# State step of an S5 and attention trunk with the chunks stationary, joined value blocks, a gate bias kept as one row, and read-out matrices built a block ahead

## The chip, the core and the metric

The kernel runs on one core of a Trainium2 chip. A time is the device time of one execution in microseconds (us). The engines are TensorE (PE: matmuls, and transposes through the matmul array), VectorE (DVE), ScalarE (ACT), GpSimd (POOL, here a DMA queue and nothing else) and SyncE (SP, a second DMA queue). PE writes into eight PSUM banks of 128 partitions by 512 fp32 values; ACT and DVE read them. The profile tells for every stretch which clock TensorE was granted, as a share of 2.4 GHz: 1.00 is 2.4 GHz, 0.50 is 1.2 GHz.

## What is computed

512 tokens of width 2048 go through two layers. Cut to what matters here:

```python
for l in range(2):
    shift, scale, gate = split(silu(c) @ w_ada[l] + b_ada[l], 3)
    h = rms_norm(x, norm_g[l]) * (1 + scale) + shift
    u, z_s, q, k, v, z_a = split(h @ w_in[l])             # six times 1024 columns
    # S5: 64 groups of 16 channels, each with a 64-dim complex diagonal state
    states = associative_scan(a_bar, b_bar @ u)           # along the 512 tokens
    y = gelu((c_mat @ states).real + d_skip * u)
    y_s = glu(y) * silu(z_s)
    # 8 heads, difference of two softmax maps, causal
    y_a = head_norm((softmax(q1 k1) - lam * softmax(q2 k2)) @ v) * silu(z_a)
    x = x + gate * (concat(y_s, y_a) @ w_out[l])
out = rms_norm(x, final_g)
```

## The kernel before

**Big matmuls.** Every weight is used in three products of split fp32 numbers (high by high, high by low, low by high). Weights come as units of 128 x 1024 values, 144 for a layer, numbered through. `stream_ahead` (L308) loads a unit on SP's queue, ACT copies its high part (`hi`), DVE subtracts that from the unit (`lo`). There are four `hi`/`lo` pairs, so a unit is split four units ahead of its use and no sooner.

**One step per unit.** `step` (L255) writes out, in this order: a phase, the split of a later unit, the copies that empty the last step's bank (`evacs`), a phase, the matmuls of this unit, a phase. In each of the three phases every background generator moves on by one `yield`; `idle(n)` is n steps of nothing. So a generator's instructions stand at a fixed place between units on each engine, and an engine that is late makes the others wait there. Nothing is reordered later.

**Order of a layer** (L1198): columns of u, blocks of values, columns of z, then for 8 heads k, q and z_a with attention running behind them, then the GLU and the output projection. In the value blocks (`v_step`, L1223) the tokens' tiles are stationary and 256 weight columns move: a unit is 48 matmuls. In u and z the weights are stationary and 512 tokens move: 24 matmuls for a unit. Units are counted from 0: layer 0 has value blocks in units 24 to 31 and z in 32 to 47, layer 1 has values in 144 to 147, u in 148 to 163, values again in 164 to 175 and z in 176 to 191. `v_out` copies four PSUM banks (list `VB`) through two buffers and stores them to `vD`. The first z column writes to bank 1, then 0, then 7.

**State part** (`s5_state_gen`, L771). The 512 tokens are 64 chunks of 8 for every group. For block j of 8 groups, 8 fp32 matmuls give the chunks' state input in bank 3: the matrix B (128 x 128 for a group) is stationary, the chunks `U` (128 x 64) move; one step later ACT copies the bank into the state array `X`. A scan over the chunks follows: jobs of ACT swap, four DVE operations, one job a step, three levels up and three down. Then `PR` is scaled (`CS_SG1`, L855), the first read-out matrices are loaded (`be`, `kD`, `u` on POOL's queue), `idle(2)`, and eight read-out steps: DVE builds `O` (three operations of 1024) and masks `Mb` (one), PE runs 16 matmuls into bank 3 or 2, one step later DVE and ACT compute the gelu of that bank, and one step after that PE turns the result by four transposes. In the order of instructions on DVE the build of block j comes ahead of the gelu of block j-1.

**Bias of the modulation.** `ada_gen` (L524) brings the rows of w_ada as a background task on SP's queue and multiplies on DVE; for the gate the bias of 2048 values is first loaded to all 128 partitions (1 MB) on POOL's queue, and `ada_out` adds PSUM and bias on DVE.

Helpers: `q.act` L126, `q.tt` L129, `q.ts` L134, `q.stt` L138, `q.dma` L141 (POOL's queue), `q.mm` L144, `q.tr` L152. An fp32 matmul is two MATMUL records in the trace, one of the split products or a transpose is one.

Of the kernel before, what the change touches and what calls it, by code (L numbers as in the profile page):

```python
# [338 lines left out]
def build(ctx, tc, io):  # L339
# [169 lines left out]
    def ada_out(l, c):  # L509
        b = bank[4]  # L510
        if c < 8:
            k0 = 4 * (c % 4)
            f_o, s_o = mod_o[l]
            bb = pc(PP_BA + 32 * l + 16 * (c // 4) + k0, 4)
            if c < 4:
                q.tt(v(s_o + k0, 4), b[:, 0:4], bb, A)
            else:
                q.tt(v(f_o + k0, 4), b[:, 0:4], bb, A)
                q.stt(v(f_o + k0, 4), v(f_o + k0, 4), 1.0, pc(PP_NG + 16 * l + k0, 4), A, M)
        else:  # L520
            g0 = gl.gate + (c - 8) * 512
            q.tt(v(g0, 512), b, v(g0, 512), A)

    def ada_gen(l, chunks, ring, per, gate=False, late=0):  # L524
# [8 lines left out]
        if gate:  # L533
            q.dma(v(gl.gate, D), io["bgate"][l].partition_broadcast(P))
# [236 lines left out]
    def s5_state_gen(l):  # L771

        o = S5[l]
        todo = got = 0
        while o.v < 8:
            yield
            if todo > o.v:
# [3 lines left out]
            if got < 8 and o.d > got and o.v >= got - 1:  # L781
# [24 lines left out]
        for (ar, ai), (br, bi) in zip(pw, pw[1:]):  # L806
# [4 lines left out]
            q.stt(bi, ar, 2.0, ai, M, M)  # L811
        jobs = []
# [7 lines left out]
        for i, job in enumerate(jobs):  # L820
            if job is None:
# [35 lines left out]
        def load_m(j):  # L857
            base = q.kD[l][16384 * j:16384 * (j + 1)]
            src = bass.AP(base.tensor, base.offset, [[16, P], [2048, 8], [1, P]])
            q.dma(o.B[j % 2].rearrange("p (g f) -> p g f", g=8), src)  # L860

        s5_load_be(l, 0, 128)
        load_m(0)
        s5_load_u(l, 0)
        yield from idle(2)
# [20 lines left out]
        for j in range(8):  # L886
            if j < 7:
                s5_load_be(l, j + 1, 128)
                load_m(j + 1)
                s5_load_u(l, j + 1)  # L890
            be = v(s5.BE[j % 2], 384).rearrange("p (f g q) -> p f g q", f=3, g=8)
            O = o.A[j % 2]
            On4 = O.rearrange("p (g s e) -> p g s e", g=8, s=8)
            T4 = o.T.rearrange("p (g s e) -> p g s e", g=8, s=8)
            pr = PR[:, 8 * j:8 * j + 8, :].unsqueeze(3).to_broadcast([P, 8, 8, 16])
            pi = PI[:, 8 * j:8 * j + 8, :].unsqueeze(3).to_broadcast([P, 8, 8, 16])
            q.tt(On4, pr, be[:, 1].unsqueeze(2).to_broadcast([P, 8, 8, 16]), M)
            q.tt(T4, pi, be[:, 2].unsqueeze(2).to_broadcast([P, 8, 8, 16]), M)
            q.tt(O, O, o.T, SUB)
# [298 lines left out]
    def layer(l):  # L1198
# [11 lines left out]
        def v_out(b, st, cb):  # L1210
            t = v2(ut_o[vn[0] % 2], 256)
            vn[0] += 1
            q.act(t, b, AF.Copy)
            q.dma(q.vD[l][st * P:(st + 1) * P, cb * 256:(cb + 1) * 256], t)

        VB = (2, 7, 0, 1, 5, 6) if l == 0 else (0, 1, 2, 7, 5, 6)

        def v_bank(st, cb):
            i = 4 * (cb - (2 if l == 0 else 1)) + st
            assert i < 4 or o.r == 8  # L1220
            return bank[VB[i % 6]][:, 0:256]

        def v_step(un, cb, kc):  # L1223
            def pe():
                wh, wl = q.unit(un)

                for st in (2, 3, 1, 0) if l > 0 and cb == 1 and kc == 0 else range(4):
                    rows3(v_bank(st, cb), st, wh, wl, range(4 * kc, 4 * kc + 4), 256, kc == 0, kc == 3)

            def evac():  # L1230
                for st in range(4):
                    v_out(v_bank(st, cb), st, cb)

            q.step(pe, evac if kc == 3 else None)
# [59 lines left out]
        if l == 0:  # L1294
# [13 lines left out]
        for cb in range(first_cb, 4):  # L1308
            for kc in range(4):
                v_step(un, cb, kc)  # L1310
# [3 lines left out]
        for j in range(8):  # L1314
            b = bank[(1, 0, 7)[j % 3]]
# [288 lines left out]
def _layout(x, c, positions, norm_g, w_ada, b_ada, w_in, w_out, ssm_a_re, ssm_a_im, ssm_b_re, ssm_b_im,  # L1604
# [13 lines left out]
    for l in range(DEPTH):  # L1618
# [5 lines left out]
        def put_v(u, cb):  # L1624
            m = wv[:, :, 256 * cb:256 * (cb + 1)].reshape(4, 4, P, 256)
            w[u:u + 4] = m.transpose(0, 2, 1, 3).reshape(4, P, 1024)
            return u + 4

        if l == 0:
# [99 lines left out]
```

## Time and profile before

| | |
|---|---|
| median of 3 runs | 1918.66 us (1918.45 to 1919.98) |
| the profiled execution | 1919.61 us, of which the span is 1917.8 us |
| PE busy | 1883.1 us, 98% of the span |
| DVE busy | 1350.5 us, 70% |
| ACT busy | 788.0 us, 41% |
| mean granted clock | 0.993 |

PE is busy nearly all the time, so each microsecond of matmul taken out, and each wait of PE taken out or put in, is a microsecond of the kernel. DVE's 70% is a mean: there are stretches in which it is full. A timeline row is the start of an instruction (or of a run of equal ones, x16 is sixteen), its duration with its tail, engine, line, operation, output and inputs, size; in square brackets how long the engine had been idle and who ended that. Matmuls overlap, so what a matmul costs is read as the distance of starts.

### The profile page before, as it was taken

What the parts mean: (1) busy time and instruction counts of PE and PEld (TensorE: products, weight loads), DVE (VectorE), ACT (ScalarE), POOL (GpSimd) and SP (SyncE); (2) the same over time, 40 slices, a digit from 0 to 9 for tenths busy, and PEclk for the clock granted to TensorE, in tenths of its full rate; (3) what the DMA queues carried; (4) which work ended last, traced back from release to release, by engine and by line L of the source; (5) the groups of instructions that cost most, each with busy time, mean ns of one, the idle gap of its engine ahead of it and who ended that gap; (6) DMA issues with size and microseconds to landing.
All of it is one profiled execution on the core that took longest, in us unless ns stands there. A gap on an engine that the chain in (4) does not pass through costs nothing.

```text
span 1917.8 us, 27929 instructions
## 1 busy us (share of the span) xinstructions
PE 1883.1 (98%) x10440; PEld 1590.0 (83%) x10440; DVE 1350.5 (70%) x2590; ACT 788.0 (41%) x1489; POOL 200.8 (10%) x316
## 2 busy tenths in 40 slices
PE   7999999999999999999999999999999999999998
PEld 4678998878888888888898899888788888888887
DVE  7747867997788887769876434797687787653444
ACT  4333234445445554322254224444355445432222
POOL 0003220230000000100001220033000000000000
PEclk8999999999999999999999999999999999999999
DMA  9967652776656865777544433377766684455233
GB/s 354 403 254 245 185 154 86 218 201 213 182 181 192 221 192 176 264 264 245 170 160 136 130 114 114 99 228 200 205 188 191 181 219 122 123 168 202 94 92 118
DMA packets 120696, 358.77 MB, mean 187 GB/s; under 512 B 32272, under 2 KB 32848, under 8 KB 118128
## 3 DMA queue, kind: packets, MB, share of 16 engines
q1 hardware_dynamic: 97776, 277.14, 45.3%
q0 software_dynamic: 22784, 79.84, 14.0%
q8 instruction: 82, 1.34, 0.3%
q14 instruction: 54, 0.44, 0.1%
HBM read 309.60 MB, written 30.54 MB: 177 GB/s over the span
## 4 chain that ended last, share of the span: by engine, by line
PE 74%; DVE 13%; DMA 6%; issue 4%; ACT 3%; POOL 0%; SPq 0%; ACTq 0%; DVEq 0%; POOLq 0%
PE bk L145 72%; DVE sb L130 4%; DVE lo L130 3%; DVE sb L139 3%; PE bk L153 2%; DMA sb<-in_wada 1%; DMA sb<-in_w 1%; DVE ss L130 1%; ACT hi L127 1%; DMA x<-in_x 1%; DMA sb<-in_ssm_d 1%; ACT sb L127 1%; DMA sb<-sb 1%; DVE sb L134 1%; DMA vD<-sd 0%
## 5 line engine op out<-in xcount | busy, mean ns | idle before, releaser
L130 DVE TENSOR_TENSOR lo<-sb,hi 128x1024 fp32r<-128x1024 f32 x288 | 351.0, 1221 | 361.5 <-ACT hi L127 339.2
L127 ACT ACTIVATE hi<-sb 128x1024 fp32r<-128x1024 f32 x288 | 303.6, 1058 | 518.7 <-PE bk L145 394.6
L145 PE MATMUL bk<-hth,hi 128*128 128x512 f32 x1280 | 513.5, 401 | 0.0
L145 PE MATMUL bk<-hth,lo 128*128 128x512 f32 x1280 | 500.9, 391 | 0.0
L145 PE MATMUL bk<-htl,hi 128*128 128x512 f32 x1280 | 500.2, 391 | 0.0
L145 PE MATMUL bk<-hi,hth 128*128 128x256 f32 (+1 forms) x1088 | 360.1, 331 | 4.4 <-ACT hth L127 4.0
L145 PE MATMUL bk<-lo,hth 128*128 128x256 f32 (+1 forms) x1088 | 356.0, 327 | 0.5 <-DVE lo L130 0.5
L145 PE MATMUL bk<-hi,htl 128*128 128x256 f32 (+1 forms) x1088 | 356.1, 327 | 0.0
L139 DVE SCALAR_TENSOR_TENSOR sb<-sb 128x512 f32<-128x512 f32 (+7 forms) x633 | 295.5, 473 | 21.4 <-DMA sb<-in_wada 2.0
L145 PEld LDWEIGHTS bk<-hth,lo 128*128 128x128 f32 x1280 | 241.3, 188 | 51.8
L145 PEld LDWEIGHTS bk<-htl,hi 128*128 128x128 f32 x1280 | 241.9, 189 | 49.2 <-issue 1.9
L145 PEld LDWEIGHTS bk<-hth,hi 128*128 128x128 f32 x1280 | 241.6, 189 | 48.7 <-issue 2.3
L130 DVE TENSOR_TENSOR sb<-sb 128x4 f32<-128x4 f32 (+8 forms) x455 | 219.3, 499 | 29.5 <-DMA sb<-sb 12.5
L145 PEld LDWEIGHTS bk<-hi,hth 128*128 128x128 f32 x1088 | 207.1, 190 | 34.5 <-issue 12.3
L145 PEld LDWEIGHTS bk<-hi,htl 128*128 128x128 f32 x1088 | 207.0, 190 | 18.2 <-DVE htl L130 0.5
L145 PEld LDWEIGHTS bk<-lo,hth 128*128 128x128 f32 x1088 | 207.3, 191 | 17.4 <-DVE lo L130 0.7
L145 PE MATMUL bk<-gt,hi 128*128 128x512 f32 x512 | 159.4, 392 | 0.0
L145 PE MATMUL bk<-sb 128*128 128x128 f32 (+6 forms) x932 | 134.1, 340 | 4.8 <-DVE sb L433 3.9
L127 ACT ACTIVATE sb<-bk,sb 128x512 f32<-128x512 f32 (+3 forms) x144 | 77.2, 540 | 137.2 <-DVE sb L134 133.7
L145 PEld LDWEIGHTS bk<-gt,hi 128*128 128x128 f32 x512 | 94.8, 188 | 18.8
L145 PE MATMUL bk<-gt,lo 128*128 128x512 f32 x256 | 99.8, 390 | 0.0
L127 ACT ACTIVATE sb<-sb 128x128 f32<-128x128 f32 (+2 forms) x163 | 62.7, 413 | 89.7 <-DVE sb L130 54.7
(116 smaller groups left out, 1700.2 us busy)
## 6 DMA issues: line engine op xcount, KB each, us to landing
sb<-in_w SPq DMA_DIRECT2D x288, 512.0 KB, 3.9
sb<-in_wada SPq DMA_DIRECT2D x185, 512.0 KB, 4.9
sb<-uD POOLq DMA_DIRECT2D x32, 256.0 KB, 5.0
ss<-kD POOLq DMA_DIRECT2D x16, 512.0 KB, 5.5
sb<-sb SPq DMA_DIRECT2D x128, 64.0 KB, 3.9
qk<-qk POOLq DMA_DIRECT2D x32, 256.0 KB, 4.0
sb<-in_be POOLq DMA_DIRECT2D x32, 192.0 KB, 4.4
x<-in_x SPq DMA_DIRECT2D x4, 1024.0 KB, 10.7
```

Of the source, the lines that this page charges most:

```text
L127: self.nc.scalar.activation(out=out, in_=in_, func=func, **kw)
L130: self.nc.vector.tensor_tensor(out=out, in0=a, in1=b, op=op)
L134: self.nc.vector.tensor_scalar(out=out, in0=a, scalar1=s1, scalar2=None, op0=op0)
L139: self.nc.vector.scalar_tensor_tensor(out=out, in0=a, scalar=s, in1=b, op0=op0, op1=op1)
L145: return self.nc.tensor.matmul(out, lhsT=l, rhs=r, start=a, stop=z)
L153: return self.nc.tensor.transpose(out, in_, self.ident)
```

## The change

Four edits.

1. **State step.** In blocks 1, 3, 5, 6, 7 of layer 0 and all blocks of layer 1 ("turned") the chunks are stationary (64 columns) and the matrix moves (128 columns), the result of two groups lying in the two halves of the partitions. It comes out turned; ACT copies bank 3 to `Y`, in the next step four transposes write it back into bank 3, and ACT copies it into `X`. A turned block takes two steps instead of one.
2. **Values.** Two neighbouring value blocks of 256 columns become one of 512, in layer 0 units 24 to 31 (one block of 512), in layer 1 units 168 to 175 (164 to 167 stay a block of 256). The lists of banks change; z begins at bank 7, then 0, then 1.
3. **Gate bias.** The bias is loaded as one row of 8 KB; DVE adds it to row 0 of the accumulator (1 x 512 for a chunk) ahead of the sum over partitions, and `ada_out` is a copy on ACT.
4. **Read-out.** The first loads stand ahead of the last two scan jobs; `build_out(0)` follows the scaling directly; `idle(2)` is gone; in the loop `build_out(j + 1)` stands behind the gelu of block j-1.

```diff
@@ s5_state_gen @@
             if half > o.v:
                 j = o.v
                 q.act(o.X[:, 8 * j:8 * j + 8, 1:65], bank[3].rearrange("p (g c) -> p g c", c=64), AF.Copy)
                 o.v = j + 1
-            if got < 8 and o.d > got and o.v >= got - 1:
+            elif todo > o.v:
+                q.act(o.Y, bank[3], AF.Copy)
+            if got < 8 and o.d > got and todo >= got - 1:
...
+            if todo > half:
+                for p in range(4):
+                    q.tr(bank[3][:, P * p:P * p + P], o.Y[:, P * p:P * p + P])
+                half = todo
+            elif j < 8 and o.u > j and o.r > j:
...
+                    u, b = U[:, g * 64:(g + 1) * 64], o.B[j % 2][:, g * P:(g + 1) * P]
+                    if j in turned:
+                        q.mm(bank[3][64 * (g % 2):64 * (g % 2) + 64, P * (g // 2):P * (g // 2) + P], u, b, True, True)
+                    else:
+                        q.mm(bank[3][:, g * 64:(g + 1) * 64], b, u, True, True)
+                        half = j + 1
...
         for i, job in enumerate(jobs):
+            if i == len(jobs) - 2:
+
+                s5_load_be(l, 0, 128)
+                s5_load_be(l, 1, 128)
+                load_m(0)
+                s5_load_u(l, 0)
...
-        yield from idle(2)
...
+        build_out(0)
...
             if j > 0:
                 gelu(j - 1)
+            if j < 7:
+                build_out(j + 1)
             yield
@@ ada_out, ada_gen @@
-            q.tt(v(g0, 512), b, v(g0, 512), A)
+            q.act(v(g0, 512), b, AF.Copy)
...
-            q.dma(v(gl.gate, D), io["bgate"][l].partition_broadcast(P))
+            q.dma(v(gl.gate, D)[0:1, :], io["bgate"][l].unsqueeze(0))
...
+                if c >= 8:
+                    a = v(aAcc, 512)[0:1, :]
+                    q.tt(a, a, v(gl.gate + (c - 8) * 512, 512)[0:1, :], A)
@@ layer @@
-        VB = (2, 7, 0, 1, 5, 6) if l == 0 else (0, 1, 2, 7, 5, 6)
+        VC = [(512, 512)] if l == 0 else [(256, 256), (512, 512)]
+        VB = (1, 7, 0, 2) if l == 0 else (1, 0, 2, 7, 5, 6)
...
-            b = bank[(1, 0, 7)[j % 3]]
+            b = bank[(7, 0, 1)[j % 3]]
```

Where the instructions stand now, at three places.

DVE around the first read-out of layer 0: `lo0` is the split of unit 48 and `lo1` that of unit 49. `128x16x31` is the last operation of a scan job, the `128x1024` rows that follow are build and mask. Before:

```order
L130 TENSOR_TENSOR ss0_1106<-ss0_1106,sb_75 128x16x31
L134 TENSOR_SCALAR sb_75<-sb_75 128x512
L130 TENSOR_TENSOR lo0_71<-sb_75,hi0_67 128x1024
L130 TENSOR_TENSOR lo1_72<-sb_75,hi1_68 128x1024
L139 SCALAR_TENSOR_TENSOR sb_75<-sb_75,bk1_77 128x512
L130 TENSOR_TENSOR ss0_1106<-sb_75 128x1024
L130 TENSOR_TENSOR sb_75<-sb_75 128x1024
L130 TENSOR_TENSOR ss0_1106<-ss0_1106,sb_75 128x1024 x2
```

and after:

```order
L130 TENSOR_TENSOR lo0_71<-sb_75,hi0_67 128x1024
L130 TENSOR_TENSOR sb_75<-ss0_1106,sb_75 128x496 x2
L130 TENSOR_TENSOR sb_75<-sb_75 128x496
L130 TENSOR_TENSOR ss0_1106<-ss0_1106,sb_75 128x16x31
L134 TENSOR_SCALAR sb_75<-sb_75 128x512
L130 TENSOR_TENSOR ss0_1106<-sb_75 128x1024
L130 TENSOR_TENSOR sb_75<-sb_75 128x1024
L130 TENSOR_TENSOR ss0_1106<-ss0_1106,sb_75 128x1024 x2
```

The last scan job stood behind the split of unit 47 and stands behind that of unit 48, and scan, scaling, build and mask are now one group without a split between them. On PE the first read-out stands behind unit 46 instead of behind unit 47, and in layer 1 behind unit 186 instead of 187.

SP's queue in layer 1 at the first two heads' rope swaps (`sb_75<-sb_75 32x512`, L1383 before, L1413 after; `in_wada` are the gate's rows). Before:

```order
L1383 DMA sb_75<-sb_75 32x512 x4
L315 DMA sb_75<-in_w 128x1024 x2
L1383 DMA sb_75<-sb_75 32x512 x4
L531 DMA sb_75<-in_wada 128x1024 x2
L315 DMA sb_75<-in_w 128x1024 x2
L531 DMA sb_75<-in_wada 128x1024 x2
```

and after:

```order
L1413 DMA sb_75<-sb_75 32x512 x4
L315 DMA sb_75<-in_w 128x1024
L531 DMA sb_75<-in_wada 128x1024 x2
L315 DMA sb_75<-in_w 128x1024
L1413 DMA sb_75<-sb_75 32x512 x4
L315 DMA sb_75<-in_w 128x1024
```

The first two rows of the gate moved from behind the second swap to a step ahead of it.

ACT at the end of layer 0's values (`sd0_99<-bk` are the copies of `v_out`, `sb_75<-bk` that of a z column). Before, the second block:

```order
L127 ACTIVATE sd0_99<-bk2_78 128x256
L127 ACTIVATE sd0_99<-bk7_83 128x256
L127 ACTIVATE sd0_99<-bk0_76 128x256
L127 ACTIVATE sd0_99<-bk1_77 128x256
L127 ACTIVATE hi0_67<-sb_75 128x1024
```

and after:

```order
L127 ACTIVATE hi3_70<-sb_75 128x1024
L127 ACTIVATE sd0_99<-bk1_77 128x512
L127 ACTIVATE sd0_99<-bk7_83 128x512
L127 ACTIVATE sd0_99<-bk0_76 128x512
L127 ACTIVATE sd0_99<-bk2_78 128x512
```

A batch of four copies is now 512 wide, and bank 7, to which the first z column writes next, is the second of them.

## Rows read from the trace of the kernel before

**Rows 1.** The page: busy time by engine

```profile
PE 1883.1 (98%) x10440; PEld 1590.0 (83%) x10440; DVE 1350.5 (70%) x2590; ACT 788.0 (41%) x1489; POOL 200.8 (10%) x316
```

**Rows 2.** Timeline of PE, start, duration, instruction: value unit and state step, layer 0

```profile
248.38 0.28 PE L145 MATMUL bk<-hi,htl 128*128 128x256 f32 x1
248.50 1.90 PE L145 MATMUL bk<-sb,ss 128*128 128x64 f32 x16
250.21 0.36 PE L145 MATMUL bk<-hi,hth 128*128 128x256 f32 x1
```

**Rows 3.** Timeline of PE: unit's end (15 starts), read-out, transposes, next unit, layer 1

```profile
1316.41 0.39 PE L145 MATMUL bk<-hth,hi 128*128 128x512 f32 x1
...
1319.58 0.39 PE L145 MATMUL bk<-hth,lo 128*128 128x512 f32 x1
1319.90 0.44 PE L145 MATMUL bk<-ss,sb 128*64 128x128 f32 x4
...
1321.80 0.66 PE L153 MATMUL bk<-sb 128*128 128x128 f32 x4
1322.21 0.48 PE L145 MATMUL bk<-hth,hi 128*128 128x512 f32 x1
```

**Rows 4.** Timelines of ACT and PE: second block of values, first z, layer 0

```profile
282.02 0.64 ACT L127 ACTIVATE sd<-bk 128x256 f32<-128x256 f32 x2
...
281.67 0.48 PE L145 MATMUL bk<-hth,hi 128*128 128x512 f32 x1
```

**Rows 5.** Timeline of DVE: two splits, then first build and mask, layer 0

```profile
360.08 2.34 DVE L130 TENSOR_TENSOR lo<-sb,hi 128x1024 fp32r<-128x1024 f32 x2
...
362.95 1.21 DVE L130 TENSOR_TENSOR ss<-sb 128x1024 f32<-128x1024 f32 x1
...
365.33 2.36 DVE L130 TENSOR_TENSOR ss<-ss,sb 128x1024 f32<-128x1024 f32 x2
```

**Rows 6.** Timeline of PE: first read-out, two waiting transposes, unit 55, layer 0

```profile
368.61 0.39 PE L145 MATMUL bk<-hth,lo 128*128 128x512 f32 x1
368.93 0.44 PE L145 MATMUL bk<-ss,sb 128*64 128x128 f32 x4
...
411.53 0.66 PE L153 MATMUL bk<-sb 128*128 128x128 f32 x4 [1.12 <-DVE sb L139]
...
422.68 0.66 PE L153 MATMUL bk<-sb 128*128 128x128 f32 x4 [3.10 <-DVE sb L139]
...
433.16 0.48 PE L145 MATMUL bk<-hth,hi 128*128 128x512 f32 x1
```

**Rows 7.** Stretches: us, busy PE, PEld, DVE, ACT, POOL, granted clock, DMA share, GB/s

```profile
368.00:432.00 64.00, 59.75 (x448) 48.90 (x448) 57.93 (x62) 27.79 (x44) 21.20 (x27) 0.97 0.77 215
424.00:427.00 3.00, 3.00 (x9) 2.32 (x8) 2.96 (x3) 2.25 (x5) 1.57 (x2) 0.50 0.04 14
1340.00:1352.00 12.00, 12.00 (x54) 9.94 (x54) 0.32 (x1) 1.06 (x1) 1.41 (x3) 1.00 1.08 274
1356.00:1362.00 6.00, 5.95 (x18) 4.71 (x18) 5.86 (x9) 1.64 (x3) 0.00 (x0) 0.50 0.72 208
```

**Rows 8.** Timelines of DVE and PE: two splits, mask, first read-out, layer 1

```profile
1262.89 2.34 DVE L130 TENSOR_TENSOR lo<-sb,hi 128x1024 fp32r<-128x1024 f32 x2
...
1268.13 2.36 DVE L130 TENSOR_TENSOR ss<-ss,sb 128x1024 f32<-128x1024 f32 x2
...
1272.54 0.44 PE L145 MATMUL bk<-ss,sb 128*64 128x128 f32 x4
```

**Rows 9.** Timelines of four engines: scores of first head, layer 1

```profile
1338.48 3.15 SPq L1383 DMA_DIRECT2D sb<-sb  x4
...
1338.98 0.56 POOL L142 DMA_DIRECT2D sb<-in_bgate  x1
...
1351.68 2.02 DVE L130 TENSOR_TENSOR sb<-sb 128x512 f32<-128x512 f32 x3 [12.00 <-DMA sb<-sb]
...
1355.60 1.41 PE L145 MATMUL bk<-qk 128*128 128x128 f32 x4 [2.92 <-DVE qk L130]
```

More of the change, by code (lines that the diff above doesn't have):

```diff
@@ L773, in s5_state_gen @@
         o = S5[l]
-        todo = got = 0
+        todo = half = got = 0
+        turned = range(8) if l > 0 else (1, 3, 5, 6, 7)
         while o.v < 8:
             yield
-            if todo > o.v:
+            if half > o.v:
                 j = o.v
@@ L811, in s5_state_gen, with load_m @@
             q.stt(bi, ar, 2.0, ai, M, M)
+        def load_m(j):
+            base = q.kD[l][16384 * j:16384 * (j + 1)]
+            src = bass.AP(base.tensor, base.offset, [[16, P], [2048, 8], [1, P]])
+            q.dma(o.B[j % 2].rearrange("p (g f) -> p g f", g=8), src)
         jobs = []
@@ L1208, in rows3, with v_out, v_bank, v_step @@
                       first and k == 0, fin and k == len(kks) - 1)
-        def v_out(b, st, cb):
-            t = v2(ut_o[vn[0] % 2], 256)
+        def v_out(b, st, c0, w):
+            t = v2(ut_o[vn[0] % 2], w)
             vn[0] += 1
             q.act(t, b, AF.Copy)
-            q.dma(q.vD[l][st * P:(st + 1) * P, cb * 256:(cb + 1) * 256], t)
-        VB = (2, 7, 0, 1, 5, 6) if l == 0 else (0, 1, 2, 7, 5, 6)
-        def v_bank(st, cb):
-            i = 4 * (cb - (2 if l == 0 else 1)) + st
+            q.dma(q.vD[l][st * P:(st + 1) * P, c0:c0 + w], t)
+        VC = [(512, 512)] if l == 0 else [(256, 256), (512, 512)]
+        VB = (1, 7, 0, 2) if l == 0 else (1, 0, 2, 7, 5, 6)
+        def v_bank(st, n):
+            i = 4 * n + st
             assert i < 4 or o.r == 8
-            return bank[VB[i % 6]][:, 0:256]
-        def v_step(un, cb, kc):
+            return bank[VB[i % 6]][:, 0:VC[n][1]]
+        def v_step(un, n, kc):
+            c0, w = VC[n]
+            nk = 1024 // w
             def pe():
                 wh, wl = q.unit(un)
-                for st in (2, 3, 1, 0) if l > 0 and cb == 1 and kc == 0 else range(4):
-                    rows3(v_bank(st, cb), st, wh, wl, range(4 * kc, 4 * kc + 4), 256, kc == 0, kc == 3)
+                for st in (2, 3, 0, 1) if l > 0 and n == 0 and kc == 0 else range(4):
+                    rows3(v_bank(st, n), st, wh, wl, range(nk * kc, nk * kc + nk), w, kc == 0, kc == KT // nk - 1)
             def evac():
                 for st in range(4):
-                    v_out(v_bank(st, cb), st, cb)
-            q.step(pe, evac if kc == 3 else None)
+                    v_out(v_bank(st, n), st, c0, w)
+            q.step(pe, evac if kc == KT // nk - 1 else None)
         def u_out(j, b):
@@ L1307, in layer @@
             un = col_units(un, b, hth, htl, evac=lambda j=j, b=b: u_out(j, b), done=int(l == 0 and j == 2))
-        for cb in range(first_cb, 4):
-            for kc in range(4):
-                v_step(un, cb, kc)
+        for n in range(len(VC)):
+            for kc in range(KT * VC[n][1] // 1024):
+                v_step(un, n, kc)
                 un += 1
         for j in range(8):
-            b = bank[(1, 0, 7)[j % 3]]
+            b = bank[(7, 0, 1)[j % 3]]
             def z_out(j=j, b=b):
@@ L1622, in _layout, with put_v @@
         wv = wi[:, 4096:5120].reshape(KT, P, 1024)
[L1624 to L1627, printed above, removed]
+        def put_v(u, c0, n):
+            nu = KT * n // 1024
+            m = wv[:, :, c0:c0 + n].reshape(nu, KT // nu, P, n)
+            w[u:u + nu] = m.transpose(0, 2, 1, 3).reshape(nu, P, 1024)
+            return u + nu
         if l == 0:
@@ L1635, in _layout @@
                     u += 1
-            first_u, first_cb = 2, 2
+            first_u, vc = 2, [(512, 512)]
         else:
-            u = put_v(u, 0)
-            first_u, first_cb = 0, 1
+            u = put_v(u, 0, 256)
+            first_u, vc = 0, [(256, 256), (512, 512)]
         for j in range(first_u, 8):
             u = put_cols(u, wi[:, j * P:(j + 1) * P])
-        for cb in range(first_cb, 4):
-            u = put_v(u, cb)
+        for c0, n in vc:
+            u = put_v(u, c0, n)
         for j in range(8):
```

35 lines of the change are left out of this document (14 added, 21 removed).

## The prediction

> **What bounds the kernel now.** I read the page first: PE is busy 1883.1 us of a span of 1917.8 [rows 1], so the bound is PE's own stream, and the questions are what the change takes out of that stream and where it makes PE wait. For the first I read distances of starts on PE's timeline, since durations overlap. A 256-wide matmul takes 0.12 us (248.38 to 248.50), the state step of 16 records 1.71 us (248.50 to 250.21) [rows 2]. A 512-wide one takes 0.2264 us (14 distances from 1316.41 to 1319.58); the 32 records of a read-out take 1.90 us (1319.90 to 1321.80), the four transposes behind it 0.41 (1321.80 to 1322.21) [rows 3]. For the second I looked for places where another engine is as full as PE. Between the scan of layer 0 and its last gelu DVE is busy 57.93 of 64 us [rows 7], and the rest is its hand-overs with ACT in the gelu; there PE waits for it twice, 1.12 and 3.10 us at gelu transposes [rows 6], after which the granted clock is at 0.50 for 3 us [rows 7]. The third view is the stall at the first scores of layer 1: DVE idles 12.00 us for the rope swap on SP's queue and PE 2.92 for DVE [rows 9], then the clock is at 0.50 from 1356 to 1362 [rows 7].
>
> The sum is made against the profiled execution, 1919.61 us, which lies 0.95 above the median of the runs.
>
> **Joined values.** A unit was 48 x 0.12 = 5.76 us and becomes 24 x 0.2264 = 5.43: 0.33 saved. Sixteen units change (8 in each layer), all on the path, as PE does nothing else meanwhile: **-5.2 us**. The row of 512-wide matmuls is from units whose weights are stationary, and in the values the tokens are, so I keep 4 to 5.5 as the range.
> The Trainium skill (TensorE: Matmul & The Clock Gate, "Back-to-back issue gap") speaks against most of this: its isolated warm gap of N/2.4 + 2.5 ns gives 109 and 216 ns, hence 5.24 and 5.18 us for a unit, and an estimate of 1 us saved in all. The same section gives a lower sustained spacing at 512. The trace has 0.12 and 0.2264, 11 ns over that gap at either width, and a fixed cost counts twice at half the width; so the sum goes by the rows.
>
> **State step.** The new matmuls are 16 records with a stationary of 64 columns and 128 moving, which is the form of the read-out's: 1.90 / 32 = 0.059 us each [rows 3], 0.95 and some 0.15 of hand-over, 1.1 us. Four transposes of 0.41 follow a step later. So 1.71 becomes 1.5, and somewhat less where the step stands behind other small matmuls and shares their hand-over: 0.2 to 0.5 saved, 0.3 taken, in 13 blocks: **-4.0 us**. If a record of the new form costs as much as the old (1.71 / 16 = 0.107), the transposes come on top and it is +5. I take the read-out's price, the same shape. The second copy by ACT (about 0.6) and the second step are covered by the units between; ACT is at 41% [rows 1]. Their price is the step by which the scan begins later, next.
>
> **Read-out ahead, layer 0.** Two things move: the scan starts and ends one step later, since the last turned block takes two steps, and `idle(2)` goes, so the first read-out stands one unit earlier on PE. Before, the mask ended at 367.7 (365.33 + 2.36) and PE came to the read-out at 368.93 [rows 5, 6]: 1.2 us to spare. The scan is a chain DVE, ACT, DVE, with DVE behind PE by several microseconds at its end, so DVE's time counts. One step later is +5.4 on DVE, minus the two splits that no longer lie ahead of the build (2.3, [rows 5]) and the z addition behind them (0.6: 362.95 - 360.08 - 2.3): the mask ends at about 370.2. PE is there at 368.84 - 5.43 = 363.4. It waits 6.8 us. Behind that point DVE stays full up to the last gelu in the same cyclic order, so the transposes of gelu 6 come when DVE has got there, at about the time of before, and the waits of 1.12 and 3.10 are mostly used up by the 6.8. But one unit of PE that stood ahead of those transposes now stands behind them: the unit that began at 433.16 [rows 6] begins 5.4 us later: **+5.4**. With a wait of such length ahead of the last units I take another stretch at half clock, as the one of 3 us behind the 3.10 us wait [rows 6, 7]: **+1.5**. Bounds: 0 to +10.
>
> **Read-out ahead, layer 1.** Same step: mask at 1268.13 + 2.36 = 1270.5, PE at 1272.54 [rows 8]. After: 1270.5 + 5.4 - 2.9 = 1273.0 against PE at 1272.45 - 5.43 = 1267.0, a wait of 6.0. Here PE did not wait for DVE at the gelu transposes, so nothing takes it back: **+6.0**; the half clock behind it, between the 1.5 us of layer 0's stretch and the 3 us of the scores' (half of 6, [rows 7]): **+2.3**. Bounds 0 to +10. The loads that now stand ahead of the last two scan jobs (matrices, chunks) have that time to land, and behind them on POOL's queue are only a z store and later loads that nobody waits for.
>
> **z's first bank, layer 0.** z column 0 writes bank 7, the second bank that `v_out` copies. ACT began these copies at 282.02, two of 256 in 0.64 [rows 4]; two of 512 cost up to double, so bank 7 is free at about 283.2, while PE came to z at 281.67. A wait of **+1.5** (0 to 2). In layer 1 the list leaves banks that are copied early, and I take nothing.
>
> **Gate bias.** DVE's four additions of 1 x 512 for each layer take the place of four of 128 x 512; covered either way. What counts is the load: in layer 1 the 1 MB of bias was issued at 1338.98, half a microsecond behind the swap [rows 9], and all DMA engines are full from 1340 to 1352 (share 1.08, 274 GB/s, [rows 7]). With 1 MB fewer and the first two gate rows (1 MB) issued a step earlier, 2 of 3.3 MB go. Scores start 3.9 us behind the swap's landing (1351.68 to 1355.60); PE could have begun at about 1352.7 (1355.60 - 2.92), so the swap must land by 1348.7, 3 us earlier; 2 MB at 274 GB/s are 7. I take the stall as gone: wait 2.9 and 6.4 us at half clock (3.2): **-6.1**.
>
> **Sum.** -5.2 - 4.0 + 5.4 + 1.5 + 6.0 + 2.3 + 1.5 - 6.1 = +1.4: 1921.0 in the scale of the profile, 1920.0 in that of the median (1921.0 - 0.95).
>
> **Rivals.**
> *A, as summed*, read-out late in both layers: 1920, own range 1914 to 1925 (the state step's 0.2 to 0.5, half clocks of 0 to 3).
> *B, DVE gets there in time.* If the chain of the scan is limited by its hand-overs with ACT and not by DVE's work, the additional step is hidden; the read-out's four terms (15.2) vanish, and the block-ahead build may take off the waits of 1.12 and 3.10 too. For it: DVE does not compute in the whole of a scan step, it also waits for the swap. Against: the two splits that stand back to back at 360.08 [rows 5] show that DVE had work waiting there. 1900 to 1905.
> *D, half of it.* The scan's delay is 2.5 to 3 us instead of 5.4, since its first jobs are short and catch up: waits of about 3 in both layers, and no lasting half clock. 1910.
> *C, the swap still queues.* The slower side: in layer 1 the rope swap's packets lie behind two gate rows issued a unit ahead, the weight unit, q/k copies and the head's values, and land after 1348.7 all the same. That keeps 2.9 of wait and 3.2 of half clock: 1926. It decides from a landing 7 us behind the last of the four issues (it is 10 now).
> *By the page's gap rule* values give 1 us in place of 5.2: A becomes 1924. Against it the two spacings above; 3 in 100.
>
> **How the numbers follow.** A 0.42, D 0.17, B 0.16, C 0.22, gap rule 0.03. A measurement of this kernel tells about 0.2% from no change, 3.84 us: faster is below 1914.8, slower above 1922.5. A lies 0.05 faster, 0.27 same, 0.10 slower; D 0.14 faster, 0.03 same; B faster; C 0.03 same, 0.19 slower; the gap rule slower. That is 0.35, 0.33, 0.32. The range 1904 to 1927 leaves out the half of B below it and the upper end of C.
>
> **What would show it.** In the changed trace: value units of 5.43 us; the turned state step near 1.1 and its transposes 0.41 a unit later; PE's waits for DVE's mask at the first read-out of both layers, 6 to 7 us, followed by a granted clock of 0.50; a wait for ACT at the first z of layer 0; no wait at the first scores of layer 1 and a clock of 1.00 there. Read-outs without a wait would make me wrong by up to 20 us; a state step of 1.7 by 9 on the other side.

## The result

The changed kernel takes 1932.57 us (median of 4 runs, 1929.12 to 1936.34) against 1918.56 for the kernel before (1917.55 to 1919.98): ratio 1.0068, 95% interval 1.0055 to 1.0081. By the medians it is slower by 14 us, where 1920 and a range up to 1927 had been forecast. The profiled execution has a span of 1930.2 us, 12.4 more than before.

The page of the changed kernel, busy time by engine and the chain that ended last:

```profile
PE 1880.2 (97%) x10108; PEld 1566.4 (81%) x10108; DVE 1350.7 (70%) x2590; ACT 799.6 (41%) x1502; POOL 196.0 (10%) x308
PE 77%; DVE 10%; issue 6%; DMA 3%; ACT 2%; POOL 0%; SPq 0%; ACTq 0%; DVEq 0%; POOLq 0%
```

PE's busy time fell by 2.9 us (1883.1 in [rows 1]), although more of it ran at a lower clock (mean granted clock 0.988, before 0.993). So on balance the loss is idle time of PE. The changed kernel's timeline of PE at the first read-out of layer 0, at the last gelu transposes there, and at the first read-out of layer 1:

```profile
371.41 0.69 PE L145 MATMUL bk<-ss,sb 128*64 128x128 f32 x4 [7.35 <-DVE ss L130]
...
433.52 0.65 PE L153 MATMUL bk<-sb 128*128 128x128 f32 x4 [2.34 <-DVE sb L139]
...
1282.25 0.69 PE L145 MATMUL bk<-ss,sb 128*64 128x128 f32 x4 [9.44 <-DVE ss L130]
```

Where [rows 6, 8] show read-outs that start right behind their unit, PE now waits 7.35 and 9.44 us for DVE's mask. The two waits of before at gelu transposes (1.12 and 3.10) have become one of 2.34. The masks end at these times, timeline of DVE:

```profile
369.00 2.36 DVE L130 TENSOR_TENSOR ss<-ss,sb 128x1024 f32<-128x1024 f32 x2
...
1279.84 2.36 DVE L130 TENSOR_TENSOR ss<-ss,sb 128x1024 f32<-128x1024 f32 x2
```

That is 371.4 in layer 0 and 1282.2 in layer 1. The stretches behind the waits, and that of the first scores of layer 1 (us, busy PE, PEld, DVE, ACT, POOL, granted clock, DMA share, GB/s):

```profile
280.00:290.00 10.00, 9.46 (x34) 7.66 (x35) 4.36 (x8) 4.88 (x8) 2.23 (x4) 0.83 0.47 159
370.00:380.00 10.00, 8.59 (x51) 7.38 (x51) 9.45 (x10) 1.71 (x3) 2.91 (x4) 0.67 0.62 179
1280.00:1290.00 10.00, 7.75 (x46) 6.66 (x47) 9.97 (x10) 1.23 (x2) 3.45 (x5) 0.60 0.54 167
1356.00:1362.00 6.00, 6.00 (x29) 4.95 (x28) 1.63 (x3) 1.78 (x3) 1.86 (x3) 1.00 1.00 278
```

The clock is below 1.00 behind each of these three waits; from 1356 to 1362, where it was 0.50 [rows 7], it is 1.00. The scores of layer 1, which began behind a wait of 2.92 us [rows 9], wait 0.70 now; the swap lands 4.5 us behind its last issue instead of 10. Timelines of SP, DVE and PE:

```profile
1356.80 3.22 SPq L1413 DMA_DIRECT2D sb<-sb  x4
...
1364.55 2.02 DVE L130 TENSOR_TENSOR sb<-sb 128x512 f32<-128x512 f32 x3 [6.89 <-DMA sb<-sb]
...
1371.24 0.44 PE L145 MATMUL bk<-qk 128*128 128x128 f32 x2 [0.70 <-DVE qk L130]
```

**Where the time went.** The start of the same weight unit was read on both timelines of PE; how much later (+) it begins in the changed kernel tells what was lost up to there. The last column has the terms of the forecast:

| stretch, from unit to unit | change within it, us | forecast, us |
|---|---|---|
| values, 16 units | -5.1 (0.32 each) | -5.2 |
| state steps of layer 0 (18 to 31), without the values | 0.0 | -4.0 with the next row |
| state steps of layer 1 (154 to 170), without the values | +0.7 | |
| first z of layer 0 (31 to 33), without the value unit | +3.1 | +1.5 |
| read-out of layer 0 (33 to 56) | +7.8 | +6.9 |
| read-out of layer 1 (176 to 196) | +12.3 | +8.3 |
| first scores of layer 1 (196 to 200) | -5.2 | -6.1 |
| all others together | -1.2 | |
| sum | +12.4 | +1.4 |

These are single profiled executions; between executions of the same code such a stretch differed by 1.6 us (e10, units 33 to 56) and 2.3 us (e6, units 200 to 240).

### The profile page after: what moved, and what is told of

The parts are those of the page before. It is cut to its first block, busy times and chain, and to the rows that moved or that the text cites. A ratio compares the mean times of both kernels' runs of the same rounds, so it can differ in the third digit from the quotient of the medians.

```text
span 1930.2 us, 27270 instructions
## 1 busy us (share of the span) xinstructions
PE 1880.2 (97%) x10108; PEld 1566.4 (81%) x10108; DVE 1350.7 (70%) x2590; ACT 799.6 (41%) x1502; POOL 196.0 (10%) x308
## 4 chain that ended last, share of the span: by engine, by line
PE 77%; DVE 10%; issue 6%; DMA 3%; ACT 2%; POOL 0%; SPq 0%; ACTq 0%; DVEq 0%; POOLq 0%
PE bk L145 75%; DVE sb L130 3%; DVE lo L130 3%; PE bk L153 2%; DVE sb L139 2%; DMA sb<-in_w 1%; DVE ss L130 1%; ACT hi L127 1%; DMA x<-in_x 1%; ACT ss L127 0%; DMA sb<-sb 0%; ACT sb L127 0%; DVE sb L134 0%; ACT sd L127 0%; DMA vD<-sd 0%
## 5 line engine op out<-in xcount | busy, mean ns | idle before, releaser
L145 PE MATMUL bk<-hi,hth 128*128 128x512 f32 (+1 forms) x960 | 338.3, 352 | 4.6 <-ACT hth L127 4.2
L145 PE MATMUL bk<-lo,hth 128*128 128x512 f32 (+1 forms) x960 | 333.5, 347 | 0.5 <-DVE lo L130 0.5
L145 PE MATMUL bk<-hi,htl 128*128 128x512 f32 (+1 forms) x960 | 333.6, 348 | 0.0
L139 DVE SCALAR_TENSOR_TENSOR sb<-sb 128x512 f32<-128x512 f32 (+8 forms) x633 | 295.9, 473 | 20.7 <-DMA sb<-in_wada 1.1
L130 DVE TENSOR_TENSOR sb<-sb 128x4 f32<-128x4 f32 (+8 forms) x463 | 224.7, 502 | 24.6 <-DMA sb<-in_ssm_d 9.9
L145 PEld LDWEIGHTS bk<-hi,hth 128*128 128x128 f32 x960 | 182.0, 190 | 40.6 <-issue 13.5
L145 PEld LDWEIGHTS bk<-hi,htl 128*128 128x128 f32 x960 | 181.9, 190 | 23.4 <-DVE htl L130 0.5
L145 PEld LDWEIGHTS bk<-lo,hth 128*128 128x128 f32 x960 | 182.2, 190 | 22.0 <-DVE lo L130 0.7
L145 PE MATMUL bk<-sb 128*128 128x128 f32 (+5 forms) x932 | 134.6, 341 | 5.3 <-DVE sb L433 4.0
L127 ACT ACTIVATE sb<-bk 128x512 f32<-128x512 f32 (+2 forms) x221 | 92.5, 451 | 22.2 <-PE bk L145 12.3
```

Source lines behind the costliest of these rows:

```text
L127: self.nc.scalar.activation(out=out, in_=in_, func=func, **kw)
L130: self.nc.vector.tensor_tensor(out=out, in0=a, in1=b, op=op)
L139: self.nc.vector.scalar_tensor_tensor(out=out, in0=a, scalar=s, in1=b, op0=op0, op1=op1)
L145: return self.nc.tensor.matmul(out, lhsT=l, rhs=r, start=a, stop=z)
```

## The experiments

All runs, with the ratio to the kernel before on the same chip and its interval. The medians of the kernel before beside them were 1919.59 us (e1, e2, e4, e5), 1918.11 (e3, e6 to e8) and 1917.82 (e9 to e12):

| run | what it is | median, us | ratio (95%) |
|---|---|---|---|
| e1_gate | before + bias as a row | 1914.21 | 0.9975 (0.9966 to 0.9985) |
| e2_vals | before + joined values | 1916.00 | 0.9985 (0.9975 to 0.9994) |
| e3_state | before + turned state step, one idle step | 1927.86 | 1.0053 (1.0036 to 1.0070) |
| e4_ahead | before + read-out ahead | 1928.62 | 1.0056 (1.0041 to 1.0071) |
| e5_idle1 | changed, one idle step back | 1929.37 | 1.0057 (1.0041 to 1.0073) |
| e6_zbank | changed, z of layer 0 from bank 5 | 1931.37 | 1.0070 (1.0052 to 1.0088) |
| e7_last | changed, last block not turned, two idle steps | 1914.66 | 0.9983 (0.9973 to 0.9992) |
| e8_last_z | the same, z of layer 0 from bank 5 | 1914.42 | 0.9980 (0.9970 to 0.9990) |
| e9_pair | before + bias and values, z's banks free | 1909.75 | 0.9958 (0.9943 to 0.9973) |
| e10_split | changed, layer 1's last value copies in two steps | 1928.76 | 1.0064 (1.0048 to 1.0081) |
| e11_pair_split | e9 with value copies in two steps | 1909.50 | 0.9958 (0.9943 to 0.9973) |
| e12_state_split | e11 + turned state step but for the last block | 1908.31 | 0.9951 (0.9937 to 0.9966) |

The theory after the result: two edits each bring the first read-out one step nearer to the end of the scan, the turned last block by starting the scan a step later, the lost idle steps (two, less the step that the scan moved) by putting the read-out a unit earlier; where the read-out comes too near, PE waits, and this lost more than the two other edits gained. Rivals: one of the two edits alone; the build ahead of the gelu; or something in ACT's queue. In the runs the read-out stands nearer to the scan's end than before by this many steps, and PE waits so long for the mask:

| steps nearer | runs | wait in layer 0, us | wait in layer 1, us |
|---|---|---|---|
| 0 | before, e1, e2, e7, e8, e9, e11, e12 | none | none |
| 1 | e3 | 2.58 | 3.67 |
| 1 | e5 | 3.37 | 6.65 |
| 2 | e4 | 6.50 | 5.73 |
| 2 | changed, e6, e10 | 7.35, 7.69, 7.35 | 9.44, 9.24, 8.13 |

### The four edits one by one

**e1_gate.** The three bias hunks of the change on the kernel before:

```diff
-            q.dma(v(gl.gate, D), io["bgate"][l].partition_broadcast(P))
+            q.dma(v(gl.gate, D)[0:1, :], io["bgate"][l].unsqueeze(0))
...
-            q.tt(v(g0, 512), b, v(g0, 512), A)
+            q.act(v(g0, 512), b, AF.Copy)
```

> The kernel before with the gate's bias as a row alone. Theory: the 1 MB load was what held the rope swap of layer 1's first head, so PE's wait of 2.9 us there and the half clock behind it go, as in the changed kernel, where 5.2 us came back at that place: about 1913. Rival: the swap was held by other transfers, or what freed it was that the gate's rows were issued a step earlier in the changed kernel: no change, 1918.5.

It came as the theory said. DVE's idle time for the swap falls from 12.00 to 8.44 us and PE's scores begin without a wait (timelines of DVE and PE; the row of before is in [rows 9]):

```profile
1347.20 2.02 DVE L130 TENSOR_TENSOR sb<-sb 128x512 f32<-128x512 f32 x3 [8.44 <-DMA sb<-sb]
...
1351.59 0.69 PE L145 MATMUL bk<-qk 128*128 128x128 f32 x4
```

The start of unit 200 lies 5.3 us earlier against unit 196. SP's order was that of before here, so the bias hunks alone did it; that the gate's first rows were also issued a step earlier was not needed.

**e2_vals.** The values' hunks of the change, banks included:

```diff
+        VC = [(512, 512)] if l == 0 else [(256, 256), (512, 512)]
+        VB = (1, 7, 0, 2) if l == 0 else (1, 0, 2, 7, 5, 6)
...
-            b = bank[(1, 0, 7)[j % 3]]
+            b = bank[(7, 0, 1)[j % 3]]
```

> The kernel before with the joined value blocks and their banks alone. Theory: 16 units at 5.43 instead of 5.76 us give 5.1 us, and the first z column of layer 0 takes back 1.3 us of wait for ACT and 1.6 us of half clock behind it: about 1916.5. Rival: the wider copies and stores also hold ACT in the scan, and DVE's mask comes late at the first read-outs: 1920 or more.

1916.00, as the theory. The 16 units give 0.32 each; then PE waits for ACT's copy at the first z of layer 0, and at the second z of layer 1, which I had not listed (timeline of PE):

```profile
280.24 0.50 PE L145 MATMUL bk<-hth,hi 128*128 128x512 f32 x1 [1.33 <-ACT sd L127]
...
1216.43 0.50 PE L145 MATMUL bk<-hth,hi 128*128 128x512 f32 x1 [0.97 <-ACT sd L127]
```

**e3_state.** The turned state step, with one idle step instead of two, so that the first read-out stands behind the same unit as before:

```diff
         s5_load_u(l, 0)
-        yield from idle(2)
+        yield from idle(1)
```

> The kernel before with the turned state step alone, and one idle step instead of two, so that the first read-out stands behind the same unit as before while the scan starts one step later. Theory: the step by which the scan comes later is paid at the first read-outs (waits of about 3.4 us in layer 0 and 6 in layer 1 with half clock behind them), the matmuls give some 2 us and waits for ACT at the state steps take 2: about 1928. Rival: the edits of the read-out alone made the waits: 1917.

1927.86. Timeline of PE, a state step of layer 0, then the first read-outs of both layers:

```profile
263.15 1.09 PE L145 MATMUL bk<-ss,sb 128*64 128x128 f32 x16 [1.75 <-ACT ss L127]
...
372.69 0.44 PE L145 MATMUL bk<-ss,sb 128*64 128x128 f32 x4 [2.58 <-DVE ss L130]
...
1281.68 0.70 PE L145 MATMUL bk<-ss,sb 128*64 128x128 f32 x4 [3.67 <-DVE ss L130]
```

Both read-outs wait, 2.58 and 3.67 us where nothing waited in [rows 6, 8], with the read-out's place unchanged. The waits are smaller than I wrote (3.4 and 6), the time is as forecast: unit 196 begins 5.2 us later against unit 170. And the state step itself waits 1.75 us: ACT's second copy stands behind value copies that wait for their stores.

**e4_ahead.** The read-out's hunks alone, the scan where it was.

```diff
-        yield from idle(2)
...
+        build_out(0)
```

> The kernel before with the read-out matrices a block ahead alone: without the idle steps the first read-out stands two units earlier on PE, the scan where it was. Theory: the place of the read-out relative to the scan's end makes PE wait, about 7 us in each layer and half clock behind it, of which layer 0 gets its old waits of 4.2 us back: plus 12 to 18, about 1933. Rival: the scan's later start, by the turned state step, made the waits, and without it DVE is in time: within 3 us of 1918.5.

1928.62, nearer to the theory than to the rival, though 4 us short of it. Timeline of PE, first read-out of layer 0, its last gelu transposes, first read-out of layer 1:

```profile
364.71 0.70 PE L145 MATMUL bk<-ss,sb 128*64 128x128 f32 x4 [6.50 <-DVE ss L130]
...
432.43 0.66 PE L153 MATMUL bk<-sb 128*128 128x128 f32 x4 [2.09 <-DVE sb L139]
...
1273.55 0.70 PE L145 MATMUL bk<-ss,sb 128*64 128x128 f32 x4 [5.73 <-DVE ss L130]
```

So neither edit alone is the cause, and each would do: by the medians the kernel with a scan one step later is 9.8 us slower (e3 against the runs beside it), that with a read-out two steps earlier 9.0, and in the changed kernel a step of each came together. The four parts add up to 9.8 us (-5.4 - 3.6 + 9.8 + 9.0), the whole is 14.0.

The difference lies in a stretch that can be won only once. In its read-outs e4 loses 14.6 us (5.2 from unit 33 to 56, 9.4 from 176 to 196), but at the first scores of layer 1 (196 to 200) it gains 6.7, with the 1 MB of bias still loaded. Timelines of POOL, SP and DVE in e4:

```profile
1342.67 0.57 POOL L142 DMA_DIRECT2D sb<-in_bgate  x1
...
1356.00 2.41 SPq L1392 DMA_DIRECT2D sb<-sb  x4
...
1361.70 2.02 DVE L130 TENSOR_TENSOR sb<-sb 128x512 f32<-128x512 f32 x3 [2.08 <-DMA sb<-sb]
```

The bias is issued 13 us ahead of the swap here, where it was half a microsecond behind it [rows 9]; DVE waits 2.08 us for the swap instead of 12.00 (and 3.94 for the one before it, which lay beside the load), and PE not at all at the scores. In the profiled executions of e1, e2, e3 and e4 this stretch is shorter by 5.3, 2.8, 2.6 and 6.7 us, 17.3 in all; in the changed kernel by 5.2.

### What the wait at the read-out is made of

**e5_idle1.** One idle step back between first build and first read-out of the changed kernel:

```diff
         build_out(0)
+        yield from idle(1)
```

> The changed kernel with one idle step put back between the first build and the first read-out, so that the read-out stands behind the same unit as before the change. Theory: PE's waits at the first read-out fall by one unit of 5.4 less a split of 1.2 and an addition: from 7.35 to about 3.5 us and from 9.4 to about 6; with less half clock the kernel gains 6 to 10 us: about 1924. Rival: DVE is what sets the end of the read-outs anyway, so a later read-out only moves the wait: 1931.

The waits did about what the theory said, the time is nearer to the rival. Timeline of PE, first read-out and last gelu transposes of layer 0, first read-out of layer 1:

```profile
374.15 0.54 PE L145 MATMUL bk<-ss,sb 128*64 128x128 f32 x4 [3.37 <-DVE ss L130]
...
431.16 0.66 PE L153 MATMUL bk<-sb 128*128 128x128 f32 x4 [3.55 <-DVE sb L139]
...
1285.12 0.70 PE L145 MATMUL bk<-ss,sb 128*64 128x128 f32 x4 [6.65 <-DVE ss L130]
```

In layer 0 the first wait is 3.37 instead of 7.35, but the gelu transposes wait again, 1.20, 1.17 and 3.55, in sum 9.3 us with the first, where the changed kernel has 9.7 (7.35 and 2.34): from unit 33 to 56 the run is only 1.1 us shorter than the changed kernel. DVE is full there [rows 7], and its end sets the time more than the place of the first read-out. In layer 1 2.8 us of wait went, and 1.9 us between units 176 and 196.

**e7_last.** The last block of each layer not turned, and the read-out behind the unit of before:

```diff
-        turned = range(8) if l > 0 else (1, 3, 5, 6, 7)
+        turned = range(7) if l > 0 else (1, 3, 5, 6)
...
         build_out(0)
+        yield from idle(2)
```

> The changed kernel with the last block of each layer not turned (4 and 7 turned blocks), so that the scan starts as early as in the kernel before, and two idle steps between the first build and the first read-out, which then stands behind the same unit as before. Theory: the later scan is what made the read-outs late; without it PE waits under 1 us at both first read-outs, the value copies of layer 1 no longer stand ahead of the swap of the scan's long step, and values, gate bias and state step keep their gains: about 1910. Rival: the build ahead of the gelu, or the earlier loads, hold DVE: waits of 3 us or more remain, 1922.

1914.66: by the medians 18 us faster than the changed kernel, 5 short of the theory. Timelines of DVE (end of the mask) and PE (first read-out of layer 0, its last gelu transposes, first read-out of layer 1):

```profile
366.33 1.22 DVE L130 TENSOR_TENSOR ss<-ss,sb 128x1024 f32<-128x1024 f32 x1
...
369.13 0.44 PE L145 MATMUL bk<-ss,sb 128*64 128x128 f32 x4
...
423.59 0.66 PE L153 MATMUL bk<-sb 128*128 128x128 f32 x4 [3.53 <-DVE sb L139]
...
1273.03 0.44 PE L145 MATMUL bk<-ss,sb 128*64 128x128 f32 x4
```

No read-out waits. Together with e3 and e4, which move one of the two alone, this settles the mechanism: the scan's start, one step, and the read-out's place. The gelu transposes wait 3.53 us as before, with the build a block ahead: that edit takes nothing off them. Of the missing 5 us, 3.2 are in the state steps of layer 1 (units 154 to 170), where one waits 2.05 us for ACT behind value copies, and the granted clock is 0.83 from 1166 to 1176.

**e6_zbank and e8_last_z.** z in layer 0 from bank 5, in the changed kernel and in e7:

```diff
-            b = bank[(7, 0, 1)[j % 3]]
+            b = bank[(5, 7, 0)[j % 3] if l == 0 else (7, 0, 1)[j % 3]]
```

> The changed kernel with the z columns of layer 0 beginning at bank 5, which the values don't use. Theory: the wait of 1.33 us for the copy and the 1.6 us of half clock behind it go: about 3 us faster than the changed kernel, 1929. Rival: they go, but what PE gains it gives back at the first read-out, since ACT's copies and the scan set DVE's time there: as the changed kernel, 1932.

> As the run with the last block not turned, and the z columns of layer 0 beginning at bank 5. Theory: another 3 us, 1907, as nothing behind it is limited by DVE then. Rival: the wait at the first z is given back at layer 0's gelu transposes: 1910.

The wait at z went in both. In e8 the rival is right: between units 18 and 33 it is 3.1 us shorter than e7, between 33 and 56 3.0 longer; PE came earlier and then waited for DVE, for a split (0.53) and at the gelu transposes of 379 us (1.75), where e7 waits 0.30. In e6 2.9 us are gained up to unit 33 and kept up to 56, with waits of

```profile
369.78 0.69 PE L145 MATMUL bk<-ss,sb 128*64 128x128 f32 x4 [7.69 <-DVE ss L130]
...
431.90 1.12 PE L153 MATMUL bk<-sb 128*128 128x128 f32 x4 [3.10 <-DVE sb L139]
```

for the 7.35 and 2.34 of the changed kernel, but other places of that execution were longer, and the medians differ by 1.2 us with intervals that overlap. So what a wait at z is worth stays between nothing and 3 us.

**e10_split.** The copies of layer 1's last value block two and two:

```diff
             def evac():
-                for st in range(4):
-                    v_out(v_bank(st, n), st, c0, w)
+                put(0, 2)
+                q.later(1, lambda: put(2, 4))
```

> The changed kernel, with the four copies of layer 1's last value block made two in one step and two in the next, so that ACT need not wait for the stores of the first two. Theory: the 5.4 us for which DVE idles in the middle of the scan of layer 1 came from ACT's swap standing behind these copies; it falls to 1 or 2, PE's wait at the first read-out of layer 1 from 9.4 to about 6, as forecast, and the kernel gains 4 to 5 us: 1928. Rival: DVE's idle time is that of PE's pace and the wait stays at 9 us: 1932.5.

This asked why layer 1's wait is 9.44 and not the 6.0 of the forecast. In the changed kernel the swap of the scan's long step (64 x 448) stands behind the four copies, two of which wait for stores. Timelines of ACT and DVE, changed kernel:

```profile
1213.95 1.07 ACT L127 ACTIVATE sd<-bk 128x512 f32<-128x512 f32 x2
1217.57 0.60 ACT L127 ACTIVATE sd<-bk 128x512 f32<-128x512 f32 x1 [2.56 <-DMA vD<-sd]
1220.13 0.60 ACT L127 ACTIVATE sd<-bk 128x512 f32<-128x512 f32 x1 [1.95 <-DMA vD<-sd]
1220.75 2.11 ACT L127 ACTIVATE ss<-ss 64x448 f32<-64x448 f32 x2
1222.88 2.01 ACT L127 ACTIVATE hi<-sb 128x1024 fp32r<-128x1024 f32 x2
...
1223.97 1.23 DVE L130 TENSOR_TENSOR lo<-sb,hi 128x1024 fp32r<-128x1024 f32 x1 [5.36 <-ACT hi L127]
```

and in the kernel before, where that swap was issued one step earlier, ahead of the copies:

```profile
1207.27 2.19 ACT L127 ACTIVATE ss<-ss 64x448 f32<-64x448 f32 x2 [4.63 <-DVE ss L130]
...
1210.46 0.64 ACT L127 ACTIVATE sd<-bk 128x256 f32<-128x256 f32 x2
...
1210.58 1.23 DVE L130 TENSOR_TENSOR lo<-sb,hi 128x1024 fp32r<-128x1024 f32 x1 [3.41 <-ACT hi L127]
```

DVE idles 5.36 us instead of 3.41. With the copies divided (timelines of DVE and PE):

```profile
1221.25 1.22 DVE L130 TENSOR_TENSOR lo<-sb,hi 128x1024 fp32r<-128x1024 f32 x1 [4.29 <-ACT hi L127]
...
1279.27 0.69 PE L145 MATMUL bk<-ss,sb 128*64 128x128 f32 x4 [8.13 <-DVE ss L130]
```

Both fall, 5.36 to 4.29 and 9.44 to 8.13, and from unit 176 to 196 the run gains 2.3 us, half of what the theory had. The whole time does not show it: the ratio, 1.0064, lies within the interval of the changed kernel (1.0055 to 1.0081), and from unit 33 to 56, where the code is the same, this execution is 1.6 us shorter too. So the copies are a part, by these rows: DVE's gap at this place is 3.3 to 3.4 us where the scan starts as before (before, e7), 4.76 behind the narrow copies of e3, 5.36 behind the wide ones. The second part is the split ahead of the last scan job of layer 1: it waits 1.36 us in the changed kernel, 2.28 in e5 and 1.02 in e10, for ACT and that for the load of its weight unit, and not at all in e3, which has the later scan and not the read-out's loads brought forward, nor in e4, which has the loads and not the later scan (there ACT's copy for a split waits 5.62 us for its unit, but DVE does not idle for it). The two together, 2.0 and 1.4 us, are the 3.4 by which the wait was underrated, and 0.6 and 2.3 are the 3.0 by which e5 waits longer than e3. That the loads brought forward delay the weight unit, and that DVE idles for it only with the later scan, is argued from this comparison; it was not tried by itself.

### A version that beats both

**e9_pair, e11_pair_split.** Bias and values on the kernel before, state step and read-out untouched, z's banks free when z writes them; in e11 all later value copies in two steps.

```diff
+            b = bank[((5, 7, 0) if l == 0 else (7, 5, 1))[j % 3]]
```

> The kernel before with the gate's bias as a row and the joined values, and z's banks 5, 7, 0 in layer 0 and 7, 5, 1 in layer 1, so that no z column writes a bank that is still being copied; state step and read-out as before. Theory: 5.4 us for the bias, 2.6 in layer 1 for the values, and in layer 0 the values' 2.6 are given back at the gelu transposes, where DVE sets the end: 8 us, 1910. Rival: the values' 5.1 come in full: 1907.5.

> As the pair of bias and values, with the copies of every later value block made two and two a step apart. Theory: splits of weights and swaps no longer stand behind a wait of ACT for stores (4 to 5 us of DVE's idle time at the start of the scan), DVE is earlier at layer 0's gelu transposes and their waits of 1.1 and 3.1 us shrink: 3 us less than the pair. Rival: the scan's own chain sets DVE's time: as the pair.

1909.75 and 1909.50. By its median e9 is as the theory, but at unit 56 it is still 2.4 us ahead: the values' gain in layer 0 isn't given back, and that part of the theory was wrong: every unit from 33 to 48 starts 2.6 us earlier, and the gelu transposes wait 0.84 and 3.62 us, much as before. The divided copies change nothing that can be measured: the rival of e11.

**e12_state_split.** e11 with the turned state step in all blocks but the last of each layer, read-out as before.

> As the run before, and the turned state step in all blocks but the last of each layer, read-out as in the kernel before. Theory: 11 turned blocks give 0.15 to 0.23 us each, about 2, and no state step of layer 1 waits for ACT behind value copies: 2 us less than without. Rival: the copies' wait (2 us at a state step of layer 1) stays, or what layer 0 gains is given back at the gelu transposes: no gain, or 2 us more.

1908.31, the lowest here; the interval overlaps e11's. Between units 154 and 170 it gains 0.8 us more than e11, 0.12 for each of seven blocks, and no state step of layer 1 waits for ACT. Between 18 and 31 it gains 0.35 against e11 and nothing against e9. So what the turned state step gives the whole time is not clear of the noise. The run is 0.49% faster than the kernel before (0.34% to 0.63%), and by the medians 24 us faster than the change.

## Why the prediction was wrong, step by step

On the profile's scale the forecast was 11.0 us too low, +1.4 for +12.4. The state step makes 4.7 of them, the read-out of layer 1 4.0 and the clock behind the first z 1.6; the others together make 0.7. The first two are the steps that failed, and neither alone would have carried 1920 past 1927. That the read-outs would come late in both layers (A) was right.

- **Joined values: right**, -5.1 for -5.2. The spacing read from weight-stationary units holds with the tokens stationary, and the isolated gap of the Trainium skill (TensorE: Matmul & The Clock Gate, "Back-to-back issue gap"), by which an estimate of 1 us would have come, does not describe it: 5.1 us came.
- **State step: the price right, the saving wrong (+0.7 for -4.0), the largest miss.** The new form takes 1.12 us (1.24 from the last unit matmul to the next, less 0.12), the transposes 0.36 (timeline of PE):

```profile
1152.20 0.60 PE L153 MATMUL bk<-sb,ss 128*128 128x128 f32 x4
1152.56 0.36 PE L145 MATMUL bk<-hi,hth 128*128 128x256 f32 x1
...
1158.26 0.28 PE L145 MATMUL bk<-hi,htl 128*128 128x256 f32 x1
1158.47 1.09 PE L145 MATMUL bk<-ss,sb 128*64 128x128 f32 x16
1159.50 0.39 PE L145 MATMUL bk<-hi,hth 128*128 128x256 f32 x1
```

That is 0.23 a block. By the starts of units a block saved that much where it stood alone between units of u (154 and 155), 0.15 in units 166 and 167, and only 0.11 to 0.13 beside other small matmuls (156 to 165), where I had put 0.2 to 0.5 for each: an estimate from these of 1.4 to 2 us for 13 blocks instead of 4. In layer 0 five turned blocks came to 0.0; PE waits 0.60 us for ACT at another small matmul there (239.59), and where the remainder went stays open. In layer 1 the saving was lost where I had called ACT's copies covered because ACT is at 41%. The mean says nothing of a queue in order: the copy of a block stands behind value copies that wait for stores (timelines of ACT and PE, layer 1):

```profile
1169.33 0.39 ACT L127 ACTIVATE sd<-bk 128x256 f32<-128x256 f32 x1 [2.17 <-DMA vD<-sd]
1172.11 0.38 ACT L127 ACTIVATE sd<-bk 128x256 f32<-128x256 f32 x1 [2.39 <-DMA vD<-sd]
1172.39 0.59 ACT L127 ACTIVATE ss<-bk 128x512 f32<-128x512 f32 x1
...
1173.03 1.10 PE L145 MATMUL bk<-ss,sb 128*64 128x128 f32 x16 [1.60 <-ACT ss L127]
```

- **First z: mechanism and wait right** (1.33 for 1.5), but unit 32 took 1.6 us longer behind it, at a granted clock of 0.50 from 282 to 284 us; I had given half clock to long waits only.

```profile
279.42 1.07 ACT L127 ACTIVATE sd<-bk 128x512 f32<-128x512 f32 x2
...
280.54 0.50 PE L145 MATMUL bk<-hth,hi 128*128 128x512 f32 x1 [1.33 <-ACT sd L127]
```

- **Read-out of layer 0: right.** Wait 7.35 for 6.8, +7.8 in all for +6.9.
- **Read-out of layer 1: the other step that failed, by its size.** The wait was forecast, but I carried the 5.4 us less 2.9 over from layer 0, as if DVE ran without a gap behind the scan's start. It had gaps for ACT (3.3 to 3.4 us in the trace of before), and they grew by 3.4 us, of which 2.0 lie behind the value copies and 1.4 at the split that waits for its unit: the wait was 9.44 for 6.0, +12.3 in all for +8.3. I had noted that ACT's copies in layer 1 end early for z, and not asked what else stands behind them in ACT's queue once the scan moves a step.
- **Scores: right**, -5.2 for -6.1, and e1 shows the mechanism on the kernel before. But e4 got as much without the bias edit, so that the edit earned these 5.2 us in the changed kernel too is not shown.
- **Rivals and range.** B and D, which had a third of the chance, named a step that is hidden or half hidden; the waits of 7.35 and 9.44 us show neither. The slower side I gave to the swap (C) and not to the waits themselves: with my own upper bound of 10 us for each layer's read-out A reaches 1925, and layer 1's 12.3 lay outside that bound, which had no row behind it. One more of DVE's gaps of 3.3 to 3.4 us in the scan of before, added to layer 1's bound, would have given 13.4 for it and 1928.

## What to carry to other kernels

When a chain on another engine ends just in time (1.2 and 2.0 us to spare here), a step's delay of its start and a step's advance of its consumer add: one step nearer cost PE a wait of 2.6 to 6.7 us, two steps 5.7 to 9.4. Ask for the spare time first. Take the delay through every in-order queue that the chain passes, here ACT's, and look what it now stands behind. In a stretch where a second engine is full, a wait removed from the first can be given back at the next hand-over (3.0 of 3.1 us in e8, but not in e6), so do not count on it. And a stall that one edit removes cannot be removed by another again: look for the same stretch in the gains of several edits before they are added.

## What was not expected of the hardware

A wait of 1.33 us at z was followed by a stretch at a lower granted clock in the changed kernel, in e2, e5 and e7 (0.83 over 280 to 290 us), but in e10 the same wait of 1.33 us left it at 1.00 (timeline of PE and the stretch):

```profile
279.99 0.50 PE L145 MATMUL bk<-hth,hi 128*128 128x512 f32 x1 [1.33 <-ACT sd L127]
...
280.00:290.00 10.00, 10.00 (x44) 8.30 (x45) 2.98 (x7) 3.53 (x5) 1.97 (x4) 1.00 0.46 159
```

Layer 0 of e10 is the changed kernel's code, and unit 32 took 1.6 us less there. So executions of the same code can differ by such a stretch; the four runs of the changed kernel spread over more than that (1929 to 1936), and why is not shown. In e2 a wait of 0.97 us at a z of layer 1 left the clock at 1.00. At state steps of layer 1 waits of 1.60 (changed kernel) and 1.65 us (e5) left it at 1.00 over the 10 us from 1170, while waits of 2.05 (e7) and 2.12 us (e10) were followed by 0.83 over 10 us.
